# An RWKV-7 chunk scan in a two-layer hybrid mixer: the triangular inverse is folded into the keys, and a step has two links instead of three

## The chip, the cores and the metric

One Trainium2 chip, one of its cores. The metric is device time of one execution in microseconds; lower is better. All 512 tokens (256 of context, 256 latent, width 2048) go through two layers in one launch.

## The reference

Each layer normalises and modulates the tokens, projects them once, runs four token mixers in parallel (A and C are attentions, B is RWKV-7 in both directions, D is a gated DeltaNet in both directions), gates and projects each, sums them, and adds an output projection. The change touches mixer B, whose recurrence is

```python
def step(s, inp):
    r_t, w_t, k_t, v_t, kk_t, a_t = inp
    sa = jnp.einsum('bhij,bhj->bhi', s, -kk_t)
    s = (s * w_t[:, :, None, :] + sa[..., None] * (kk_t * a_t)[:, :, None, :]
         + v_t[..., None] * k_t[:, :, None, :])
    return s, jnp.einsum('bhij,bhj->bhi', s, r_t)
```

run over the context and then the latent tokens, forward and backward, for eight heads of 64, all in float32. The outputs of the context are needed in the first layer only.

## The kernel before

**Two kinds of TensorE work.** The large products (projections, branch merges, output projection) are split into high and low halves and run as 128x128 matmuls of 512 or 256 columns into PSUM tiles named `big`, with weights `wh`, `wl` that ScalarE and VectorE split from the loaded `wr`. These are the *fills*. They sit in a queue of generators, `s.queue`, and are drawn from it while other work is emitted. The planner is `small` (L259): each small matmul that the program emits reports a price in ns (`mm`, L282, and `turn`, L299), the price times `rho` is added to a debt, and as soon as the debt is above zero fills are emitted until it is paid and at least `QUANT` = 2600 ns of them stand there. A scheduler of the framework then sets the final order on each engine by dependences.

**The RWKV scan.** The tokens are cut into eight chunks of 64. Within a chunk the recurrence is solved with a unit triangular 64x64 inverse. Heads go in four pairs `j`; one head of a pair lies in partitions 0 to 63, the other in 64 to 127, so every tile holds both, and each 64x64 matmul uses one corner quarter of the array. For each pair and direction `d`, `b_stage1` (L886) builds per chunk: `ar` (decayed keys and receptances), the products `AT01`, `AT10`, `AT11` (L948 to 963), `tok0` and `tok1` (keys with tokens in the partitions, `tok2` L796) and the matrix to be inverted. `b_scan` (L971) then runs eight steps, one for a chunk, with the state `S`:

- link 1: `Z = AT10.vt + ar.S` in PSUM (tile `sc`), copied to SBUF by VectorE (L991);
- link 2: `U = E.Z` with the inverse `E` (tile `iR`), copied by VectorE (L997);
- link 3: `S' = wc * (tok1.vt + tok0.U) + wc * S`, VectorE L315 (L319 in the first step), the last term by ScalarE (`sw`, L309);
- beside these, the output is accumulated over the whole scan in a PSUM tile `acc`: `vt.AT11`, `S.ar`, `U.AT01`, for the chunks whose output is needed.

There are 4 pairs x 2 directions x 8 steps in each layer, 128 steps in all. Matmuls are written head by head (`for R in HS`).

**The inverse.** `inv_gen` (L704) is a generator that yields after each operation: 31 pairs of VectorE operations `it`, `iX` (L715, L717) on 32x32 blocks, two VectorE transposes `iE` and `iF` (L723, L725), 16 matmuls `iF,iL`, ScalarE copies to `iT` and POOL copies, 16 matmuls of `iT` and `iE`, ScalarE copies into `iR`. The inverse of the direction that comes next is run in the background of a scan: `bgstep(n)` (L677) advances it by n operations, after link 1, after link 2 and at the end of a step by `BG` = 3, 3, 4, and `bgstep(1000)` behind the scan finishes it. The DeltaNet mixer uses the same `inv_gen`.

Of the kernel before, what the change touches and what calls it, by code (L numbers as in the profile page):

```python
# [183 lines left out]
STEP = 1050.0  # L184
BG = (3, 3, 4, 10, 10)


class Kern:
    def __init__(s, tc, ins, out, dbg=None):
        s.tc, s.nc, s.i, s.out = tc, tc.nc, ins, out  # L190
        s.n = s.l = 0
        s.queue, s.done, s.debt, s.rho, s.filling, s.bg = [], set(), 0.0, 0.0, False, []
        s.side, s.sdebt, s.inside = None, 0.0, False
        s.wide, s.form = 0.0, (128, 128)


    def nm(s, t):
        s.n += 1
        return f"{t}_{s.n}"

    BUFS = {t: 2 for t in ("ar AT01 AT10 AT11 tok0 tok1 wc bo vt dl nb dec Dk ktok vs pT pt aq "
                           "iR sw po it").split()}
    BUFS.update(mr=16, Z=3, U=3, S=3, vs=3, dZ=3, Sd=4, Rb=16, po=3, ms=1, wr=5, wh=4, wl=4, QD=3, qg=3, dl=4, vn=2,
                nb=4, dec=4)
# [54 lines left out]
    def small(s, ns):  # L259
        if s.filling:  # L260
            s.wide += ns
            return
        if s.side and not s.inside:
            s.sdebt += ns * SIDE[s.l]
            while s.sdebt > 0 and s.side:
                s.sdebt -= STEP
                s.sidestep()
        s.debt += ns * s.rho
        if s.debt > 0:
            got = 0.0  # L270
            while s.queue and (s.debt > 0 or got < QUANT):
                s.pump()
                s.debt -= s.wide
                got += s.wide
# [7 lines left out]
    def mm(s, o, l, r, start=True, stop=True):  # L282
        s.nc.tensor.matmul(o, l, r, start=start, stop=stop)  # L283
        k, m, n = l.shape[0], l.shape[-1], int(np.prod(r.shape[1:]))
        if l.dtype == F32R:
            ns = max(n / 2.4 + 13, 107)
        elif k == m == 128:
            ns = max(4 * n / 2.4, 222)
        elif m == 32 and k == 128:
            ns = n / 2.4  # L290
        elif m <= 32:
            ns = 52
        elif k == m:
            ns = max(1.1 * n, 60)
        else:
            ns = max(1.3 * n, 110)
        s.small(ns + s.turn(max(32, k), max(32, m)))
# [406 lines left out]
    def inv_gen(s, pool, st, sign, grp, R, pair=False):  # L704
# [3 lines left out]
        nc = s.nc  # L708
        Bt, X, lo = st
        x = X.rearrange("p m i -> p i m")  # L710
# [18 lines left out]
        ps = s.bank()  # L729
# [23 lines left out]
        yield  # L753
        for D_, h, u0, u1, du, wE in out:
            up, dn = HQ[h]
            for u in range(u0, u1):
                if wE:
# [37 lines left out]

    def tok2(s, x, pool, tag):  # L796

# [3 lines left out]
        pv = ps.rearrange("p (m h f) -> p m h f", m=4, h=2)  # L801
        o = s.tl(pool, [128, 8, 64], tag)
        ov = o.rearrange("p (m e) f -> p m e f", e=2)
# [82 lines left out]
    def b_stage1(s, J, d):  # L886
# [59 lines left out]
        inv = s.inv_load(pool, ps)  # L946
        AT = [[None, None], [None, None]]
        for q, x in enumerate((bt, kt)):  # L948
            for e in range(1 - q, 2):
                AT[q][e] = s.tl(pool, [128, 8, 64], "AT%d%d" % (q, e))  # L950
            for g in range(2):
# [9 lines left out]
                for e in es:  # L961
                    mk = rep(s.c("bm", d * 128 + e * 64, d * 128 + e * 64 + 64), 4)
                    s.tt(AT[q][e][:, 4 * g:4 * g + 4, :], ps[:, :, e, :], mk, ALU.mult)
        tok = [s.tok2(x, pool, "tok%d" % q) for q, x in enumerate((bt, kt))]
        E = s.tl(pool, [128, 8, 64], "iR")
        J["d"][d] = (ar, AT, tok, E, wc)
        s.background(s.inv_gen(pool, inv, -1, [(0, 8, d == 1)], E))

    ORDER = [[0, 1, 2, 3, 4, 5, 6, 7], [3, 2, 1, 0, 7, 6, 5, 4]]

    def b_scan(s, J, d):  # L971
        nc = s.nc
        pool, t0 = s.bst["pool"], s.bst["t0"]
        c0 = t0 // 64
        ar, AT, tok, E, wc = J["d"][d]
        vt = J["vt"]
# [3 lines left out]
        yps = J["y"]  # L980
        pc = None
        S = None
        for st in range(8):
            c = s.ORDER[d][st]
            ps = s.scb((128, 64))
            for R in HS:
                s.mm(ps[R, :], AT[1][0][R, c, :], vt[R, c, :], True, st == 0)
                if st > 0:
                    s.mm(ps[R, :], ar[R, c, 0, :], S[R, :], False, True)
            Z = s.tl(pool, [128, 64], "Z")  # L990
            nc.vector.tensor_copy(Z, ps)  # L991
            s.bgstep(BG[0])
            ps = s.scb((128, 64))
            for R in HS:
                s.mm(ps[R, :], E[R, c, :], Z[R, :])
            U = s.tl(pool, [128, 64], "U")
            nc.vector.tensor_copy(U, ps)  # L997
            s.bgstep(BG[1])
            Sn = None
            if st < 7:  # L1000
                ps = s.scb((128, 64))
                for R in HS:
                    s.mm(ps[R, :], tok[1][R, c, :], vt[R, c, :], True, False)
                    s.mm(ps[R, :], tok[0][R, c, :], U[R, :], False, True)
                Sn = s.tl(pool, [128, 64], "S")
# [6 lines left out]
            if c >= c0:  # L1012
                for R in HS:
                    o = yps[R, c * 64:c * 64 + 64]
                    s.mm(o, vt[R, c, :], AT[1][1][R, c, :], d == 0 and c == c0, False)
                    if st > 0:
                        s.mm(o, S[R, :], ar[R, c, 1, :], False, False)
                    s.mm(o, U[R, :], AT[0][1][R, c, :], False, d == 1 and st == 7)
            s.bgstep(BG[2])
            S = Sn  # L1020
# [580 lines left out]
```

## Time and profile before

| | |
|---|---|
| median of 3 runs | 2846.87 us (2844.48 to 2854.17) |
| profiled execution | 2842.45 us |
| its span in the trace | 2840.7 us, mean granted clock 0.984 |
| RWKV scans of layer 0 | 244.9 to 737.0 us of the span |
| RWKV scans of layer 1 | 1803.0 to 2205.0 us of the span |

The span is that of the profiled execution, from the first to the last instruction in the trace. In the rows, PE is TensorE, DVE is VectorE, ACT is ScalarE, PEld a weight load. A name such as `sc<-Z,iR` says that a matmul wrote a tile `sc` from the tiles `Z` and `iR`; L283 is the line of the helper that records every matmul, so matmuls are told apart by their tiles. An fp32 matmul leaves two records. The end of a matmul's record is modelled, so what it costs is read from the distance of the starts.

### The profile page before, as it was taken

Reading aid. Unit: us, or ns where it says so; the run is one execution under the profiler, and the core shown is the slowest. Engines: PE = TensorE matmul, PEld = TensorE weight load, DVE = VectorE, ACT = ScalarE, POOL = GpSimd, SP = SyncE. Lnnn points to the kernel's source line nnn. Section 1 sums busy time; section 2 is a strip of 40 time slices with the busy share of each in tenths; the row PEclk is TensorE's granted clock in tenths of the full one; section 3 lists DMA queues with packets and bytes.
Section 4 is the critical chain, followed back from the end, with each engine's and each line's share of the span. In section 5 each row is a group of like instructions: output and inputs, shape, how many; then the busy total and the mean of one; then the engine's idle time right before and its main releaser. Section 6 shows DMA issues by size and latency. Waiting matters only on the chain. (4 is left out here: it accounts for less than half of the span.)

```text
span 2840.7 us, 52626 instructions
## 1 busy us (share of the span) xinstructions
PE 2710.4 (95%) x19438; PEld 2056.8 (72%) x19438; DVE 1856.9 (65%) x5255; ACT 1260.0 (44%) x2705; POOL 180.0 (6%) x436
## 2 busy tenths in 40 slices
PE   7998999999999998999999999999999999999897
PEld 3676666677787786777787756776777887867897
DVE  4337776656676777876553354777765687678775
ACT  3334333333354555655442244444443356455553
POOL 0000000000010101000000000010010001100000
PEclk9999999999999999999999999999999999999999
DMA  9753243322342323224537886322332442433465
GB/s 346 261 189 127 83 131 105 127 83 68 115 121 88 100 72 115 79 82 134 170 114 248 279 282 203 96 78 78 93 91 75 157 143 88 133 98 88 144 190 159
DMA packets 210049, 385.80 MB, mean 136 GB/s; under 512 B 24640, under 2 KB 37824, under 8 KB 209792
## 3 DMA queue, kind: packets, MB, share of 16 engines
q1 hardware_dynamic: 199872, 351.23, 39.6%
q0 software_dynamic: 9920, 31.20, 2.9%
q8 instruction: 153, 2.51, 0.4%
q14 instruction: 104, 0.85, 0.1%
HBM read 346.95 MB, written 35.39 MB: 135 GB/s over the span
## 5 line engine op out<-in xcount | busy, mean ns | idle before, releaser
L283 PE MATMUL big<-Rb,wh 128*128 128x512 f32 (+1 forms) x3280 | 1100.7, 364 | 21.3 <-ACT Rb L1325 10.0
L283 PE MATMUL big<-Ra,wh 128*128 128x512 f32 (+1 forms) x2128 | 777.3, 365 | 8.9 <-DVE po L315 5.6
L375 ACT CAST wh<-wr 128x512 fp32r<-128x512 f32 x712 | 438.8, 619 | 762.8 <-PE big L283 576.2
L283 PEld LDWEIGHTS big<-Rb,wh 128*128 128x128 f32 x3280 | 612.1, 191 | 128.8 <-ACT Rb L1325 14.0
L312 DVE TENSOR_TENSOR wl<-wr,wh 128x512 fp32r<-128x512 f32 x712 | 488.4, 688 | 304.3 <-ACT wh L375 280.3
L283 PE MATMUL big<-Ra,wl 128*128 128x512 f32 (+1 forms) x1616 | 597.2, 370 | 6.3 <-DVE wl L312 6.3
L283 PEld LDWEIGHTS big<-Ra,wh 128*128 128x128 f32 x2128 | 407.5, 192 | 84.3 <-issue 9.5
L283 PE MATMUL big<-Rb,wl 128*128 128x512 f32 (+1 forms) x1088 | 380.4, 350 | 1.1 <-DVE wl L312 1.1
L283 PEld LDWEIGHTS big<-Ra,wl 128*128 128x128 f32 x1616 | 310.3, 192 | 53.4 <-DVE wl L312 8.6
L283 PEld LDWEIGHTS big<-Rb,wl 128*128 128x128 f32 x1088 | 207.6, 191 | 26.2 <-DVE wl L312 1.5
L312 DVE TENSOR_TENSOR iX<-iX,it 128x60 f32<-128x60 f32 (+24 forms) x744 | 181.4, 244 | 15.7
L312 DVE TENSOR_TENSOR it<-iB,iX 128x60 f32<-128x60 f32 (+24 forms) x744 | 172.7, 232 | 15.6
L315 DVE SCALAR_TENSOR_TENSOR po<-po,big 128x512 f32<-128x512 f32 (+1 forms) x128 | 70.6, 552 | 77.1 <-PE big L283 74.2
L283 PE MATMUL big<-Rb,wr 128*128 128x256 f32 (+1 forms) x448 | 111.3, 417 | 5.0 <-ACT po L309 3.1
L309 ACT ACTIVATE sw<-S,wc 128x64 f32<-128x64 f32 x96 | 33.4, 348 | 176.2 <-DVE S L315 153.5
L283 PE MATMUL big<-mr,s 128*32 128x512 f32 x384 | 85.2, 617 | 18.3 <-DMA mr<-in_wmod 18.3
L309 ACT ACTIVATE po<-big,gb 128x512 f32<-128x512 f32 (+1 forms) x128 | 74.2, 579 | 57.3 <-PE big L283 41.2
L283 PEld LDWEIGHTS big<-Rb,wr 128*128 128x128 f32 (+1 forms) x448 | 70.6, 179 | 24.1 <-issue 7.3
L283 PE MATMUL sc<-vt,AT 64*64 64x64 f32 x512 | 71.3, 238 | 0.0
L315 DVE SCALAR_TENSOR_TENSOR cz<-raw,par,cz 128x508 f32<-128x508 f32 (+3 forms) x96 | 67.2, 700 | 5.4 <-ACT cz L309 5.0
L632 DVE TENSOR_REDUCE mx<-mx 128x1 f32<-128x512 f32 (+1 forms) x96 | 57.1, 599 | 18.7 <-PE mx L283 17.5
L283 PE MATMUL sc<-vt,tok 64*64 64x64 f32 x448 | 67.5, 232 | 0.0
(371 smaller groups left out, 4033.0 us busy)
## 6 DMA issues: line engine op xcount, KB each, us to landing
wr<-in_win SPq DMA_DIRECT2D x440, 256.0 KB, 2.7
mr<-in_wmod SPq DMA_DIRECT2D x320, 256.0 KB, 5.0
wr<-in_wbr SPq DMA_DIRECT2D x128, 256.0 KB, 2.7
wr<-in_wout SPq DMA_DIRECT2D x128, 256.0 KB, 3.1
wr<-in_wmod SPq DMA_DIRECT2D x64, 256.0 KB, 3.9
wr<-in_gup SPq DMA_DIRECT2D x64, 256.0 KB, 2.6
x<-in_xT SPq DMA_DIRECT2D x16, 256.0 KB, 5.4
po<-y SPq DMA_DIRECT2D x16, 256.0 KB, 3.0
```

The lines of the kernel that those rows point to most:

```text
L283: s.nc.tensor.matmul(o, l, r, start=start, stop=stop)
L309: s.nc.scalar.activation(o, i, f, bias=bias, scale=scale, **k)
L312: s.nc.vector.tensor_tensor(o, a, b, op)
L315: s.nc.vector.scalar_tensor_tensor(o, a, sc, b, op0, op1)
L375: s.nc.scalar.copy(hi, raw)
L632: nc.vector.tensor_reduce(mx[:, hc], ps[:, 0:nk], AX.X, ALU.max)
```

## The change

Since U is only used linearly, `tok0.U = (tok0.E).Z` and `U.AT01 = Z.(E.AT01)`. A new generator `b_fold` makes the inverse in the transposed form `F` (same tile name, `iR`), then multiplies it once into `TA`, a tile that holds `tok0` and `AT01` side by side: 16 matmuls of 64x64 by 128 columns for a pair and direction (64 columns for chunks without output), evicted by ScalarE into `TA` itself. A step then has two links: Z, and S straight from Z by `TA`. U, its copy and the product E.Z are gone. The matmuls of the two heads are written in turns, in the scan and in the second block of `inv_gen`. `held` keeps the planner from emitting fills except at two places of a step. The background inverse advances by 5 and 5 instead of 3, 3 and 4. The planner's price of a 64x64 matmul of n columns goes from 1.1 n (at least 60) to 0.85 n (at least 30) ns.

```diff
-BG = (3, 3, 4, 10, 10)
+BG = (5, 5, 0, 10, 10)
...
@@ small
-        if s.debt > 0:
+        if s.debt > 0 and not s.held:
@@ mm
-            ns = max(1.1 * n, 60)
+            ns = max(0.85 * n, 30)
@@ inv_gen
-        for D_, h, u0, u1, du, wE in out:
-            up, dn = HQ[h]
-            for u in range(u0, u1):
+        a, b = [[(u, wE) for _, g, u0, u1, _, wE in out if g == h for u in range(u0, u1)] for h in range(2)]
+        for z in zip(a, b):
+            for (up, dn), (u, wE) in zip(HQ, z):
                 if wE:
                     s.mm(p2[dn, u, :], T1[up, u, :], E[up, u, :])
                 else:
...
@@ b_stage1
-        AT = [[None, None], [None, None]]
+        TA = s.tl(pool, [128, 8, 2, 64], "TA")
+        AT = [[None, TA[:, :, 1, :]], [s.tl(pool, [128, 8, 64], "AT1%d" % e) for e in range(2)]]
...
-        tok = [s.tok2(x, pool, "tok%d" % q) for q, x in enumerate((bt, kt))]
-        E = s.tl(pool, [128, 8, 64], "iR")
-        J["d"][d] = (ar, AT, tok, E, wc)
-        s.background(s.inv_gen(pool, inv, -1, [(0, 8, d == 1)], E))
+        s.tok2(bt, pool, None, TA[:, :, 0, :])
+        tok1 = s.tok2(kt, pool, "tok1")
+        J["d"][d] = (ar, AT[1], TA, tok1, wc)
+        s.background(s.b_fold(pool, inv, d, TA, c0))
+
+    def b_fold(s, pool, inv, d, TA, c0):
+
+        F = s.tl(pool, [128, 8, 64], "iR")
+        yield from s.inv_gen(pool, inv, -1, [(0, 8, d == 0)], F)
+        for _ in range(5):
+            yield
+        for g in range(2):
+            w = 2 if 4 * g >= c0 else 1
+            ps = s.bank((128, 4, 2, 64))
+            for cc in range(4):
+                for R in (slice(0, 64), slice(64, 128)):
+                    s.mm(ps[R, cc, 0:w, :], F[R, 4 * g + cc, :], TA[R, 4 * g + cc, 0:w, :])
+            s.nc.scalar.copy(TA[:, 4 * g:4 * g + 4, 0:w, :], ps[:, :, 0:w, :])
+            yield
@@ b_scan
+            o = lambda R: yps[R, c * 64:c * 64 + 64]
+            s.held = True
             ps = s.scb((128, 64))
             for R in HS:
-                s.mm(ps[R, :], AT[1][0][R, c, :], vt[R, c, :], True, st == 0)
-                if st > 0:
+                s.mm(ps[R, :], AT[0][R, c, :], vt[R, c, :], True, st == 0)
+            if st > 0:
+                for R in HS:
                     s.mm(ps[R, :], ar[R, c, 0, :], S[R, :], False, True)
             Z = s.tl(pool, [128, 64], "Z")
             nc.vector.tensor_copy(Z, ps)
-            s.bgstep(BG[0])
-            ps = s.scb((128, 64))
-            for R in HS:
-                s.mm(ps[R, :], E[R, c, :], Z[R, :])
-            U = s.tl(pool, [128, 64], "U")
-            nc.vector.tensor_copy(U, ps)
-            s.bgstep(BG[1])
-            Sn = None
             if st < 7:
                 ps = s.scb((128, 64))
                 for R in HS:
-                    s.mm(ps[R, :], tok[1][R, c, :], vt[R, c, :], True, False)
-                    s.mm(ps[R, :], tok[0][R, c, :], U[R, :], False, True)
+                    s.mm(ps[R, :], tok1[R, c, :], vt[R, c, :], True, False)
+            if c >= c0:
+                for R in HS:
+                    s.mm(o(R), vt[R, c, :], AT[1][R, c, :], d == 0 and c == c0, False)
+                if st > 0:
+                    for R in HS:
+                        s.mm(o(R), S[R, :], ar[R, c, 1, :], False, False)
+            s.bgstep(BG[0])
+            s.held = False
+            s.small(0.0)
+            s.held = True
+            Sn = None
+            if st < 7:
+                for R in HS:
+                    s.mm(ps[R, :], TA[R, c, 0, :], Z[R, :], False, True)
                 Sn = s.tl(pool, [128, 64], "S")
...
             if c >= c0:
                 for R in HS:
-                    o = yps[R, c * 64:c * 64 + 64]
-                    s.mm(o, vt[R, c, :], AT[1][1][R, c, :], d == 0 and c == c0, False)
-                    if st > 0:
-                        s.mm(o, S[R, :], ar[R, c, 1, :], False, False)
-                    s.mm(o, U[R, :], AT[0][1][R, c, :], False, d == 1 and st == 7)
-            s.bgstep(BG[2])
+                    s.mm(o(R), Z[R, :], TA[R, c, 1, :], False, d == 1 and st == 7)
+            s.bgstep(BG[1])
+            s.held = False
+            s.small(0.0)
             S = Sn
```

The omitted rest lets `tok2` write into a given tile, sets `held` up and gives `TA` two buffers.

How instructions move, at three places. The first is one step of the last scan of layer 0 on TensorE, from Z to the next Z (`sc` and `acc` are the PSUM tiles of the links and the output, `big` the fills). Before:

```order
L283 MATMUL sc_7720<-Z_7718,iR_7196 64x64 x2
L283 MATMUL sc_7725<-vt_6234,tok_1661_7191 64x64
L283 MATMUL acc_7197<-AT_1649_7117,vt_6234 64x64
L283 MATMUL acc_7197<-ar_7012,S_7689 64x64
L283 MATMUL big_7592<-Ra_1536,wh_7759 128x512
L283 MATMUL sc_7725<-U_7723,tok_1659_7181 64x64
L283 MATMUL sc_7725<-vt_6234,tok_1661_7191 64x64
L283 MATMUL sc_7725<-U_7723,tok_1659_7181 64x64
L283 MATMUL acc_7197<-AT_1641_7076,U_7723 64x64
L283 MATMUL acc_7197<-AT_1649_7117,vt_6234 64x64
L283 MATMUL acc_7197<-ar_7012,S_7689 64x64
L283 MATMUL acc_7197<-AT_1641_7076,U_7723 64x64
```

After:

```order
L283 MATMUL sc_7417<-vt_5975,AT_1517_6777 64x64 x2
L283 MATMUL acc_6898<-AT_1518_6778,vt_5975 64x64 x2
L283 MATMUL big_7439<-Ra_490,wl_7443 128x512
L283 MATMUL sc_7417<-S_7411,ar_6715 64x64 x2
L283 MATMUL sc_7424<-vt_5975,tok_1536_6893 64x64 x2
L283 MATMUL acc_6898<-ar_6715,S_7411 64x64 x2
L283 MATMUL big_7439<-Ra_498,wh_7442 128x512
L283 MATMUL sc_7424<-Z_7422,TA_6776 64x64 x2
L283 MATMUL acc_6898<-TA_6776,Z_7422 64x64 x2
L283 MATMUL big_7439<-Rb_499,wh_7442 128x512
```

The two matmuls with U into `sc` and into `acc` are gone, the row of `Z,iR` has become one of `Z,TA`, and rows that named one head at a time now come as x2, one for each head.

The second place is the end of an inverse in layer 1 on TensorE (`iF,iL` and the product of `iE` and `iT` are its two blocks of matmuls, `wr`, `wh` and `wl` are weights of fills). Before, where the first `sc<-Z,iR` follows 36 rows below the last one shown:

```order
L283 MATMUL mx_20788<-iF_20765,iL_20311 32x32 x16
L283 MATMUL mx_20934<-cst_87,raw_20932 128x2 x4
L283 MATMUL big_21019<-Rb_17702,wr_21017 32x512
L283 MATMUL big_21019<-Rb_17710,wr_21017 32x512
L283 MATMUL big_21019<-Rb_17718,wr_21017 32x512
L283 MATMUL big_21019<-Ra_17725,wr_21017 32x512
L283 MATMUL mx_20788<-iE_20764,iT_20789 32x32 x16
L283 MATMUL big_21019<-Ra_17733,wr_21017 32x512
```

After:

```order
L283 MATMUL mx_21178<-iF_21167,iL_20770 32x32 x16
L283 MATMUL big_21640<-Ra_17557,wl_21853 128x512
L283 MATMUL big_21640<-Ra_17565,wh_21852 128x512
L283 MATMUL big_21640<-Rb_17566,wh_21852 128x512
L283 MATMUL big_21640<-Ra_17565,wl_21853 128x512
L283 MATMUL mx_21178<-iE_21166,iT_21179 32x32 x16
L283 MATMUL big_21640<-Ra_17573,wh_21852 128x512
L283 MATMUL big_21640<-Rb_17574,wh_21852 128x512
L283 MATMUL big_21640<-Ra_17573,wl_21853 128x512
L283 MATMUL mx_21257<-TA_20781,iR_20879 64x64 x8
L283 MATMUL mx_21267<-TA_20781,iR_20879 64x128 x8
L283 MATMUL mx_21299<-raw_21295,cb_17958 128x256
L283 MATMUL sc_21568<-Z_21566,TA_20781 64x64 x2
```

Behind the inverse now stand the two groups of the fold, `mx<-TA,iR`, and right behind them the first link of the scan that reads it.

The third place is VectorE in a step of a scan in layer 0, from Z to the next link (`it` and `iX` are the steps of the background inverse). Before:

```order
L991 COPY Z_7321<-sc_7297 128x64
L312 TENSOR_TENSOR iX_7074<-iX_7074,it_7368 128x15x5
L312 TENSOR_TENSOR it_7376<-iB_7072,iX_7074 128x70
L312 TENSOR_TENSOR iX_7074<-iX_7074,it_7376 128x14x5
L312 TENSOR_TENSOR it_7412<-iB_7072,iX_7074 128x65
L312 TENSOR_TENSOR iX_7074<-iX_7074,it_7412 128x13x5
L312 TENSOR_TENSOR it_7415<-iB_7072,iX_7074 128x60
L312 TENSOR_TENSOR iX_7074<-iX_7074,it_7415 128x12x5
L997 COPY U_7331<-sc_7328 128x64
```

After:

```order
L1010 COPY Z_6936<-sc_6931 128x64
L312 TENSOR_TENSOR it_7000<-iB_6772,iX_6774 128x63
L312 TENSOR_TENSOR iX_6774<-iX_6774,it_7000 128x21x3
L312 TENSOR_TENSOR it_7003<-iB_6772,iX_6774 128x60
L312 TENSOR_TENSOR iX_6774<-iX_6774,it_7003 128x20x3
L312 TENSOR_TENSOR it_7006<-iB_6772,iX_6774 128x76
L312 TENSOR_TENSOR iX_6774<-iX_6774,it_7006 128x19x4
L312 TENSOR_TENSOR it_7017<-iB_6772,iX_6774 128x72
L312 TENSOR_TENSOR iX_6774<-iX_6774,it_7017 128x18x4
L312 TENSOR_TENSOR it_7020<-iB_6772,iX_6774 128x68
L315 SCALAR_TENSOR_TENSOR S_6973<-sc_6938,wc_6026,sw_6974 128x64
```

The next link's operation is the copy of U before and the S of the step after; seven operations of the inverse stood between, and now nine do.

## Rows read from the trace of the kernel before

**Rows 1.** The page, part 1: busy us, share of span, instructions by engine.

```profile
PE 2710.4 (95%) x19438; PEld 2056.8 (72%) x19438; DVE 1856.9 (65%) x5255; ACT 1260.0 (44%) x2705; POOL 180.0 (6%) x436
```

**Rows 2.** Windows of both layers' scans: us, busy (x) by engine, PEclk, DMA.

```profile
244.90:737.00 492.10, 481.00 (x4492) 332.34 (x4491) 322.59 (x1032) 170.75 (x375) 34.09 (x76) 0.99 0.32 101
1803.00:2205.00 402.00, 393.85 (x3957) 294.95 (x3958) 281.66 (x946) 167.99 (x379) 35.24 (x78) 0.97 0.28 84
```

**Rows 3.** Waits of TensorE, whole span: total us, times, longest.

```profile
PE mx L283 <- DVE iF L725: 18.6, 8, 4.7
...
PE sc L283 <- DVE Z L991: 0.9, 1, 0.9
```

**Rows 4.** Order of time, TensorE, 708.3 to 712.1: start, us, instruction.

```profile
708.50 0.27 PE L283 MATMUL sc<-S,ar 64*64 64x64 f32 x1
708.50 0.27 PE L283 MATMUL sc<-vt,AT 64*64 64x64 f32 x1
708.60 0.22 PE L283 MATMUL sc<-S,ar 64*64 64x64 f32 x1
...
708.67 0.28 PE L283 MATMUL sc<-S,ar 64*64 64x64 f32 x2
708.88 0.50 PE L283 MATMUL big<-Rb,wh 128*128 128x512 f32 x1
709.21 0.39 PE L283 MATMUL big<-Ra,wl 128*128 128x512 f32 x1
709.44 0.40 PE L283 MATMUL big<-Ra,wh 128*128 128x512 f32 x1
...
709.90 0.40 PE L283 MATMUL big<-Ra,wl 128*128 128x512 f32 x1
710.23 0.33 PE L283 MATMUL sc<-Z,iR 64*64 64x64 f32 x4
710.40 0.28 PE L283 MATMUL sc<-vt,tok 64*64 64x64 f32 x2
710.51 0.28 PE L283 MATMUL acc<-AT,vt 64*64 64x64 f32 x2
```

**Rows 5.** Windows of one scan in each layer, columns as in rows 2.

```profile
705.30:734.28 28.98, 28.93 (x286) 19.60 (x283) 8.54 (x27) 5.78 (x12) 0.54 (x1) 1.00 0.19 56
2176.66:2201.72 25.06, 25.06 (x251) 18.44 (x248) 8.69 (x26) 6.45 (x14) 1.08 (x2) 1.00 0.26 74
```

**Rows 6.** Order of time, TensorE, 2064.5 to 2066: fills of 256 columns.

```profile
2064.85 0.28 PE L283 MATMUL big<-Ra,wl 128*128 128x256 f32 x1
2064.97 0.28 PE L283 MATMUL big<-Ra,wh 128*128 128x256 f32 x1
```

**Rows 7.** Order of time, TensorE, 269.9 to 273: both blocks of one inverse.

```profile
269.98 0.69 PE L283 MATMUL mx<-iF,iL 32*32 32x32 f32 x32
...
271.73 1.09 PE L283 MATMUL mx<-iT,iE 32*32 32x32 f32 x32
```

**Rows 8.** Order of time, TensorE, 320 to 345: 16 matmuls of 128 columns.

```profile
337.10 1.96 PE L283 MATMUL mx<-ar,E 64*64 64x128 f32 x32
```

**Rows 9.** Lines by form, ScalarE: count, busy us, mean ns, idle before.

```profile
L658 ACT COPY pT<-mx 128x512 f32<-128x512 f32 x32 | 18.6, 582 | 7.4 <-PE mx L305 6.7
```

**Rows 10.** Lines by form, VectorE, columns as in rows 9.

```profile
L997 DVE COPY U<-sc 128x64 f32<-128x64 f32 x128 | 28.5, 223 | 49.9 <-PE sc L283 48.2
...
L312 DVE TENSOR_TENSOR it<-iB,iX 128x60 f32<-128x60 f32 x72 | 18.0, 250 | 1.8
```

**Rows 11.** Waits of TensorE in layer 1's scans, columns as in rows 3.

```profile
PE mx L283 <- DVE iF L725: 5.1, 4, 3.3
```

**Rows 12.** Order of time, all engines, 433 to 436: iF and its reader.

```profile
433.29 0.45 DVE L725 STREAM_TRANSPOSE iF<-iE 128x256 f32<-128x256 f32 x1
...
435.13 0.43 PE L283 MATMUL mx<-iF,iL 32*32 32x32 f32 x14
```

**Rows 13.** Window behind the longest of these waits, columns as in rows 2.

```profile
1805.00:1817.30 12.30, 12.30 (x100) 10.16 (x96) 6.21 (x13) 7.26 (x16) 1.52 (x4) 0.50 0.33 110
```

More of the change, by code (lines that the diff above doesn't have):

```diff
@@ L193, in __init__ @@
         s.side, s.sdebt, s.inside = None, 0.0, False
-        s.wide, s.form = 0.0, (128, 128)
+        s.wide, s.form, s.held = 0.0, (128, 128), False
     def nm(s, t):
@@ L199, in nm @@
         return f"{t}_{s.n}"
-    BUFS = {t: 2 for t in ("ar AT01 AT10 AT11 tok0 tok1 wc bo vt dl nb dec Dk ktok vs pT pt aq "
+    BUFS = {t: 2 for t in ("ar TA AT10 AT11 tok1 wc bo vt dl nb dec Dk ktok vs pT pt aq "
                            "iR sw po it").split()}
@@ L794, in inv_gen, with tok2 @@
                 s.act(R[H0, u0:u1, 64:128], ps[H0, u0:u1, :], AF.Copy, float(-sign))
-    def tok2(s, x, pool, tag):
+    def tok2(s, x, pool, tag, o=None):
         ps = s.bank()
@@ L801, in tok2 @@
         pv = ps.rearrange("p (m h f) -> p m h f", m=4, h=2)
-        o = s.tl(pool, [128, 8, 64], tag)
+        if o is None:
+            o = s.tl(pool, [128, 8, 64], tag)
         ov = o.rearrange("p (m e) f -> p m e f", e=2)
@@ L946, in b_stage1 @@
         inv = s.inv_load(pool, ps)
-        AT = [[None, None], [None, None]]
+        TA = s.tl(pool, [128, 8, 2, 64], "TA")
+        AT = [[None, TA[:, :, 1, :]], [s.tl(pool, [128, 8, 64], "AT1%d" % e) for e in range(2)]]
         for q, x in enumerate((bt, kt)):
-            for e in range(1 - q, 2):
-                AT[q][e] = s.tl(pool, [128, 8, 64], "AT%d%d" % (q, e))
             for g in range(2):
@@ L974, in b_scan @@
         c0 = t0 // 64
-        ar, AT, tok, E, wc = J["d"][d]
+        ar, AT, TA, tok1, wc = J["d"][d]
         vt = J["vt"]
@@ L980, in b_scan @@
         yps = J["y"]
-        pc = None
         S = None
```

## The prediction

> **What bounds the kernel now.** I began with the page's busy shares: TensorE is busy 95% of the span, VectorE 65%, ScalarE 44% [rows 1]. So anything that takes time off TensorE shows, and anything taken off another engine shows only where TensorE waits for it. The edit lies in the RWKV scans, so the next view was the two stretches that hold them, 492 us in layer 0 and 402 us in layer 1, 894 us together [rows 2]: there TensorE is busy 98%, VectorE 66 and 70%, ScalarE 35 and 42%. The third view was TensorE's waits [rows 3]. The dependent links of the scan, which one would think the reason for shortening a step from three links to two, cost TensorE almost nothing: its largest total wait for one of them is 0.9 us, for Z, in the whole program. The background inverse costs more, 18.6 us in eight waits for iF. So a shorter chain is worth nothing by itself here, because fills stand between the links. What can be won is TensorE time: fewer small matmuls, better paired ones, and fewer places where they cut into the fills.
>
> The last view was the order of time on TensorE, which prices these [rows 4]. A 64x64 fp32 matmul shows as two records. Records of the two heads (upper and lower half of the partitions) start together: at 708.50 two stand beside each other. One head's matmuls that stand alone follow at 0.11 to 0.12 us (710.40 to 710.51), so a matmul costs 117 ns alone and half, 58.5 ns, when its twin of the other head runs beside it. A fill of 512 columns follows the one before it at 0.23 us (709.21 to 709.44; 0.227 over long runs). An **interruption** of the fills by small matmuls costs more than its matmuls: the first small one starts 0.33 us after the last fill (709.90 to 710.23), 0.10 too late; the first two records are 0.10 apart (708.50 to 708.60), 0.04 too much; the last record of a stretch is at 708.73 (the second of the x2), and the fill comes at 708.88, 0.09 too late; and the next fill follows after 0.33 (708.88 to 709.21), 0.10 too late. Together 0.33 us.
>
> **The scan's matmuls.** With these prices I split one scan of each layer, both free of inverse work on TensorE [rows 5]; of the 286 and 251 records there, four stand at the edges and are left out. Layer 0: 28.98 us hold 60 fills (13.6 us), 20 interruptions (6.6) and 111 small matmuls (222 records), for which 8.8 us are left: 79 ns each. Layer 1: 25.06 us hold 25 fills of 512 columns and 48 of 256 (0.12 us each, [rows 6]), 11.4 us, 22 interruptions (7.3) and 87 matmuls in 6.4 us: 73 ns each. So the order of before, head by head, already runs half beside each other. By the order listing the scans issue 960 small matmuls in layer 0 and 784 in layer 1, afterwards 832 and 656: the 256 of E and Z are gone. Before: 960 x 79 + 784 x 73 ns = 133.0 us. After, heads strictly in turn, 1488 x 58.5 ns = 87.0 us. The difference is **-46.0 us**, of which 128 x 117 ns = 15.0 us is the removed link and the rest turn-taking. If turn-taking paired them only as well as now, 1488 matmuls at 76 ns would leave -20; that is the other bound.
>
> This rests on two heads running side by side although both write one PSUM tile, as in the rows at 708.50 (both into sc). The Trainium skill, "TensorEngine Tiling (Array Packing)", section "Gotcha 1: PSUM Pressure", states the opposite: different row tiles cannot access the same PSUM bank simultaneously. By that rule the alternating matmuls would queue at the price of lone ones; the trace disagrees with its equal starts at 708.50, so the row decides, and what the rule would give stands with the rivals.
>
> **The inverse halves.** Where the heads alternate, 32 records take 0.69 us; where eight of one head stand before eight of the other they take 1.09 [rows 7]. The second block of the inverse now alternates: 16 inverses x 0.40 = 6.4 us, and for the eight of the DeltaNet, which only partly have this shape, 0.2 us each: **-8.0 us** (bounds -6.4 and -9.6).
>
> **The fold.** New are 128 pairs of matmuls F x TA, 96 pairs of 128 columns and 32 of 64. The nearest row is the same shape, 16 matmuls, so eight pairs, of 128 columns in 1.96 us [rows 8], less the 0.16 us by which the last one's record outlasts its slot: 0.225 us a pair. 96 x 0.225 + 32 x 0.117 = **+25.3 us**. Its evictions on ScalarE, 24 of 128x512 at 0.58 us [rows 9] and 8 of half that, add 17 us to 339 of 894 busy [rows 2]: hidden, since the second group's matmuls and fills stand behind the first group's. If that cover were gone, half of the 32 would be on the path, 9 us.
>
> **The interruptions.** The planner holds the fills to two places in a step instead of three or four. Counted in the order listing, stretches of small matmuls between fills fall from 211 to 160 in layer 0's scans and from 221 to 164 in layer 1's: 108 fewer, x 0.33 = **-35.6 us** (0.23 if a quarter to a third of the loss stays with the longer stretches: -25). The planner's lower price for a small matmul also lets 222 fills leave the scans for later places; the fills are the same in number and cost the same there, so I take nothing for them. No DMA and no POOL operation is added or moved past another; the weight loads follow the fills.
>
> So far -64.3 us.
>
> **What VectorE does with it.** 128 copies of U go, 223 ns each [rows 10]: 28.5 us that nobody waited for, so nothing directly. But the inverse that VectorE computes for the next direction now has to be *folded* before that direction's first Z,TA, and TensorE gets there sooner. In layer 1, four of the eight inverses already make TensorE wait, 5.1 us together, 3.3 of it once [rows 11]. TensorE's scan there shortens by 3.8 us (per scan, matmuls 2.3, interruptions 2.4, inverse 0.4, fold back 1.4), VectorE's only by its eight U copies, 1.8 us. So up to 2.0 us of every scan's gain can turn into a wait: 8 x 2.0 = 16 us. In layer 0 the room is larger, 1.4 us after iF's end at the tightest I looked at (433.74 to 435.13, [rows 12]); with 4.1 us gained and 1.8 given by VectorE I take 0.7 us for seven inverses, 5 us. Behind that the order has only three or four fills between iF,iL and iE,iT, and three between that and the fold; ScalarE's copies between them just about fit, and I take 0.2 us at 15 places, 3 us. Together **+24 us**. The bounds are 0 (VectorE's queue runs ahead, as it does where TensorE keeps it waiting: 48.2 us ahead of the 128 copies of U [rows 10]) and 15 x 3.3 us, the longest such wait in these scans [rows 11], 50 us.
>
> That longest wait has a tail: after it, from 1805.0 to 1817.3, the granted clock is 0.50, the 1.2 GHz level [rows 13]. A tail of 12.3 us at half speed costs 6 us. I take two thirds of one more, **+4 us** (0 to 14).
>
> **Sum.** -46.0 - 8.0 + 25.3 - 35.6 + 24 + 4 = -36.3 us. The profiled execution took 2842.45 us, 1.75 more than its span, so it would come to 2806. The median of the runs is 4.4 us above it; on that scale I predict **2811 us**.
>
> **Rivals.** A change under 0.3%, 8.5 us, can't be told from none in this kernel.
>
> *The inverse stays hidden.* VectorE, relieved of U, finishes in time, and the term of 28 us falls away: 2846.87 - 64.3 = 2783. For it: 30 to 34% of VectorE is free. Against it: four waits in layer 1 already. Chance 0.12.
>
> *The inverse takes all.* Every one of 15 inverses makes TensorE wait 3.3 us, 50 us, with tails of 14: 64 of 64 are gone, 2847, within 0.3%. For it: fold and inverse now stand in a row with few fills between. Against it: the 3.3 us is the largest of eight. Chance 0.12.
>
> *Slower: the queue of VectorE.* Five inverse operations of about 0.25 us ([rows 10]) are now issued per link, where it were three or four, 3.3 on average, and the order listing has as many as nine between a Z and its S: on average a result leaves VectorE 0.4 us later. Between a link's last matmul and the first that waits for it stand two pairs (0.23), an interruption (0.33) and at least one or two fills (0.23 each), 0.8 to 1.0 us; the link itself needs 0.28 for the last record and 0.23 for the copy. That leaves 0.3 to 0.5 us for the queue. It decides when what is queued takes more than that in most links. If 224 links then expose 0.25 us each, 56 us come back on top of the forecast's -36: 2867. Against it: VectorE waits for TensorE ahead of the U copies, 48.2 us in all [rows 10], so its queue is often empty. Chance 0.07.
>
> *Heads don't run side by side in one bank.* At 117 ns each, 1488 matmuls cost 174.1 us instead of 133.0 (+41), the fold 50.6, the inverse gains nothing, and -35.6 remains: 2903. The rows at 708.50 speak against it. By the rule of the Trainium skill named above it would come out so. Chance 0.01.
>
> That the links aren't really removed can be left out: the order listing holds no U.
>
> **The numbers.** The forecast keeps 0.68; its own range is 2796 to 2830, from the bounds of the interruption term (+10), the inverse waits (+-12) and turn-taking (some +10). All of it is faster by over 0.3%. Faster: 0.68 + 0.12 = 0.80. Same: 0.12. Slower: 0.07 + 0.01 = 0.08. The range goes from 2782 to 2848, so that half of either middle rival (0.06 each) and the slower ones (0.08) lie outside: 0.20.
>
> **What would show it.** In the profile after: a small matmul of the scan costs about 60 ns in such windows, instead of 73 to 79, and the records of the two heads start in pairs throughout; TensorE's waits on iF, and new ones on TA or Z behind the fold, grown from 5 to about 25 us in the scans; the two scan stretches shorter by some 36 us in all once the fills moved out are counted back. It would be wrong if TensorE waited for Z or S by more than a few us (then VectorE's queue is the bound), if the granted clock stood at 0.50 for more than one or two further stretches, or if the waits for iF stayed at 5 us and the time fell below 2790.

## The result and the profile after

The changed kernel takes 2815.43 us (median of 4 runs, 2803.45 to 2820.73), the kernel before, measured beside it, 2845.68. The medians are 30 us apart; the ratio, which goes by the means, is 0.9882, with a 95% interval of 0.9843 to 0.992: a gain of 1.2%, some 33 us. Forecast were 2811 us.

The profiled execution took 2812.09 us, its span is 2810.3. Part 1 of its page (to be read against [rows 1]; instructions of each engine, busy us and share):

```profile
PE 2667.1 (95%) x19438; PEld 2035.5 (72%) x19438; DVE 1834.1 (65%) x5127; ACT 1277.1 (45%) x2737; POOL 180.0 (6%) x436
```

TensorE is busy 43.3 us less and the span is 30.4 us shorter, so it stands idle for 12.9 us more: 143.2 us instead of 130.3. VectorE lost its 128 copies, ScalarE gained 32 evictions and 17 us, as worked out. The mean clock of each run stands in the view of the cores (span and mean granted clock of TensorE); before it was 0.984:

```profile
core 0: 2810.3 us, clock 0.976
```

These two views split the result. Idle time is span less busy time. What the clock cost is about (1 - mean granted clock) x span, if a microsecond at half clock does half a microsecond's work: 45.5 us before, 67.4 after. (Rows for that stand below: fills of 512 columns follow each other at 0.43 us where the clock is 0.50, against 0.23.) What is left of the busy time is **TensorE's work at full clock**: 2710.4 - 45.5 = 2664.9 us before, 2667.1 - 67.4 = 2599.7 after. So the change takes 65.2 us of work off TensorE, and gives back 12.9 in idle time and 21.9 in clock: -30.4. The forecast was -64.3, +24 and +4.

The split is less sure than its decimals. The kernel before was run 27 more times beside the later experiments, with granted clocks of 0.976 to 0.981, never 0.984. By those its clock cost 59.8 us in the mean, and its idle time and work together came to 2777 to 2789 us, where its profiled execution has 2795.2. The changed kernel's four runs have 68.9 and 2743.1. By all these runs the change takes 41.9 us off idle time and work together and gives back 9.1 in clock. So what is said below of work, idle time and clock against the kernel before, from its one profile, can be wrong by some 10 us. For every other kernel here, idle time and work together in the profile lie within 6 us of the mean of its runs.

What TensorE waits for (total us, times, longest; [rows 3] and [rows 11] before):

```profile
PE mx L283 <- DVE iF L725: 35.3, 19, 4.7
...
PE sc L283 <- DVE Z L1010: 3.6, 4, 1.4
```

The waits for iF have nearly doubled from 18.6 us, and those for a link remain small. The same view of the scans alone, first of layer 0 (248.6 to 674 us), then of layer 1 (1775.5 to 2165.7):

```profile
PE mx L283 <- DVE iF L725: 4.0, 5, 1.4
```

```profile
PE mx L283 <- DVE iF L725: 15.2, 8, 2.8
```

Every one of layer 1's eight inverses now makes TensorE wait, and five of layer 0's. Before, it was four of layer 1's, for 5.1 us [rows 11]. The clock in the two scans (windows; columns as in [rows 2]: us, then busy time of PE, PEld, DVE, ACT, POOL, then PEclk) and in three of the stretches at such waits, the first of them behind an inverse of the DeltaNet:

```profile
248.60:674.00 425.40, 409.27 (x4321) 287.39 (x4316) 299.58 (x947) 168.38 (x370) 31.61 (x73) 1.00 0.34 106
1775.50:2165.70 390.20, 372.67 (x3925) 284.89 (x3926) 274.91 (x899) 172.14 (x391) 36.04 (x77) 0.94 0.28 83
```

```profile
1062.80:1083.30 20.50, 15.85 (x127) 11.82 (x128) 9.69 (x31) 9.10 (x23) 5.13 (x15) 0.50 0.39 116
2035.60:2056.10 20.50, 19.93 (x163) 14.28 (x164) 5.04 (x22) 4.09 (x10) 3.46 (x8) 0.50 0.15 46
2141.40:2151.70 10.30, 10.07 (x110) 7.53 (x110) 1.46 (x4) 3.34 (x8) 2.06 (x5) 0.50 0.24 69
```

Layer 0's scans are 67 us shorter than before, but 156 of their fills left for later places (by the listing, 1000 before, 844 now), some 35 us; layer 1's clock fell from 0.97 to 0.94. The three stretches, of 20.5, 20.5 and 10.3 us, stand at 0.50, the 1.2 GHz level; they begin late in waits of 3.63, 2.75 and 2.37 us for iF. In the trace's record of the clock, nine of the 15 stretches at 0.50 begin within 2 us of such a wait, 92 us in all; before it was five of 13, 44 us. This is the order of time around the last of the three (all engines; start, us, and in brackets idle time and its releaser):

```profile
2141.17 0.41 DVE L725 STREAM_TRANSPOSE iF<-iE 128x256 f32<-128x256 f32 x1
...
2141.63 1.06 PE L283 MATMUL mx<-iF,iL 32*32 32x32 f32 x32 [2.37 <-DVE iF L725]
...
2142.74 0.74 ACT L744 COPY iT<-mx 32x256 f32<-32x256 f32 x2 [4.72 <-PE mx L283]
...
2143.22 0.63 PE L283 MATMUL big<-Rb,wh 128*128 128x512 f32 x1
...
2143.65 0.63 PE L283 MATMUL big<-Ra,wl 128*128 128x512 f32 x1
...
2144.63 1.07 PE L283 MATMUL mx<-iT,iE 32*32 32x32 f32 x32
...
2147.20 2.83 PE L283 MATMUL mx<-TA,iR 64*64 64x64 f32 x32
...
2149.82 0.42 PE L283 MATMUL sc<-Z,TA 64*64 64x64 f32 x4
```

The chain of the inverse, iF, two blocks, fold and first link, is complete 8 us after iF, and TensorE waits only at its head: the few fills in between cover ScalarE's copies. And these rows, from a scan without inverse work, show the price of the new order (TensorE, order of time):

```profile
2156.13 0.33 PE L283 MATMUL sc<-S,ar 64*64 64x64 f32 x4
2156.30 0.28 PE L283 MATMUL sc<-vt,tok 64*64 64x64 f32 x4
2156.51 0.50 PE L283 MATMUL big<-Rb,wh 128*128 128x512 f32 x1
2156.84 0.40 PE L283 MATMUL big<-Ra,wl 128*128 128x512 f32 x1
2157.17 0.33 PE L283 MATMUL sc<-Z,TA 64*64 64x64 f32 x4
2157.34 0.28 PE L283 MATMUL sc<-vt,AT 64*64 64x64 f32 x4
2157.55 0.50 PE L283 MATMUL big<-Ra,wh 128*128 128x512 f32 x1
```

Rows come as x4 now: two heads of two records each. The 12.51 us from the fill at 2152.45 to the one at 2164.96 hold 20 fills of 512 columns (4.5 us), 12 interruptions (4.0, at the price of before) and 66 small matmuls, for which 4.0 us are left: 61 ns each, where [rows 5] gave 73. The 16 matmuls of one fold of layer 0 take 1.9 us, as their neighbour in [rows 8]:

```profile
648.91 1.92 PE L283 MATMUL mx<-TA,iR 64*64 64x128 f32 x32
```

### The profile page after: what moved, and what is told of

Same layout as the page of the kernel before. It is cut to its first block, busy times and chain, and to the rows that moved or that the text cites. A ratio compares the mean times of both kernels' runs of the same rounds, so it can differ in the third digit from the quotient of the medians.

```text
span 2810.3 us, 52526 instructions
## 1 busy us (share of the span) xinstructions
PE 2667.1 (95%) x19438; PEld 2035.5 (72%) x19438; DVE 1834.1 (65%) x5127; ACT 1277.1 (45%) x2737; POOL 180.0 (6%) x436
## 5 line engine op out<-in xcount | busy, mean ns | idle before, releaser
L309 ACT ACTIVATE po<-big,gb 128x512 f32<-128x512 f32 (+1 forms) x128 | 74.0, 578 | 68.5 <-PE big L283 52.7
L632 DVE TENSOR_REDUCE mx<-mx 128x1 f32<-128x512 f32 (+1 forms) x96 | 57.0, 598 | 20.8 <-PE mx L283 19.9
L283 PE MATMUL mx<-pT,avt 128*64 128x128 f32 x640 | 62.1, 292 | 1.5 <-ACT pT L658 1.3
L305 PE MATMUL mx<-cst,pt 128*128 128x128 f32 x320 | 52.9, 286 | 7.8 <-ACT pt L309 7.5
```

The lines of the kernel that those rows point to most:

```text
L305: s.nc.tensor.transpose(o, i, s.c("id"))
L309: s.nc.scalar.activation(o, i, f, bias=bias, scale=scale, **k)
L632: nc.vector.tensor_reduce(mx[:, hc], ps[:, 0:nk], AX.X, ALU.max)
```

## The experiments

My theory: TensorE's work sets the time, by three terms (heads in turns -39; the removed link, its interruptions and the fold together -25), and VectorE's inverse with the clock behind it gives some back. The rivals: the shorter chain is what pays; or the hold on the fills; or VectorE's queue takes over. For all runs the split of above, from page and view of the cores of the profiled execution (in us; the kernel before was measured again beside each set, 2845.7 to 2847.1; a run's median and its profiled execution differ by up to 14 us). The last two columns go by span and clock of every run of a kernel: what the clock cost in the mean, and what is left of the span, idle time and work together.

| kernel | median | ratio, interval | idle | clock cost | work | clock cost, all runs | idle and work, all runs |
|---|---|---|---|---|---|---|---|
| before | 2845.7 to 2847.1 | | 130.3 | 45.5 | 2664.9 | 59.8 | 2785.0 |
| the change | 2815.4 | 0.9882 (0.9843 to 0.992) | 143.2 | 67.4 | 2599.7 | 68.9 | 2743.1 |
| turns_only | 2811.8 | 0.9881 (0.9858 to 0.9905) | 123.3 | 56.2 | 2630.2 | 57.6 | 2753.3 |
| turns_held | 2821.5 | 0.9916 (0.9891 to 0.9941) | 128.0 | 67.6 | 2620.4 | 73.4 | 2747.7 |
| after_heads | 2845.6 | 0.9995 (0.9979 to 1.0012) | 140.3 | 88.4 | 2621.4 | 80.8 | 2763.0 |
| after_bg10 | 2798.1 | 0.9817 (0.9788 to 0.9847) | 128.0 | 41.7 | 2612.8 | 56.6 | 2736.7 |
| after_bg10_gap | 2811.0 | 0.9888 (0.9866 to 0.9911) | 142.3 | 53.2 | 2602.0 | 70.3 | 2738.7 |
| turns_gap | 2822.5 | 0.9922 (0.9896 to 0.9948) | 126.1 | 59.1 | 2629.9 | 68.5 | 2754.0 |
| after_gap7 | 2811.7 | 0.9888 (0.9858 to 0.9918) | 139.3 | 67.3 | 2598.6 | 77.4 | 2735.3 |
| after_unheld | 2787.1 | 0.9794 (0.9779 to 0.9808) | 128.9 | 55.7 | 2602.0 | 54.3 | 2731.5 |
| unheld_price | 2802.9 | 0.9847 (0.9829 to 0.9865) | 130.5 | 64.4 | 2605.5 | 61.6 | 2739.8 |
| unheld_price_bg10 | 2813.4 | 0.9881 (0.9862 to 0.99) | 135.2 | 67.4 | 2606.6 | 68.2 | 2742.6 |
| after_short | 2715.2 | 0.9539 (0.9525 to 0.9553) | 99.3 | 21.7 | 2589.5 | 26.5 | 2687.4 |
| turns_short | 2750.5 | 0.9661 (0.9647 to 0.9676) | 93.3 | 19.2 | 2634.5 | 22.0 | 2726.7 |

**One part alone: the turns.** Kernel before, `b_scan` with one loop over the heads for each operand, and the `zip` in `inv_gen`:

```diff
             for R in HS:
                 s.mm(ps[R, :], AT[1][0][R, c, :], vt[R, c, :], True, st == 0)
-                if st > 0:
+            if st > 0:
+                for R in HS:
                     s.mm(ps[R, :], ar[R, c, 0, :], S[R, :], False, True)
...
                     s.mm(ps[R, :], tok[1][R, c, :], vt[R, c, :], True, False)
+                for R in HS:
                     s.mm(ps[R, :], tok[0][R, c, :], U[R, :], False, True)
```

> The kernel before with the heads written in turns in the scan's matmuls and in the second block of the inverse; three links, planner and background as before. Theory (TensorE time by pairing): 1744 small matmuls at 58.5 instead of 76 ns, -31 us, and the inverse -8, the same number of interruptions (432 stretches): 2846 - 39 = 2807, up to 2820 if waits for the inverse give some back. Rival (the gain comes from the shorter chain): no change, 2843 to 2850. Rival (one bank serialises the heads): slower, 2880 or more.

2811.8 us: the order of the heads alone gives as much as the whole change. Work falls by 34.7 us against the profile of before (39 expected), and idle time and work together by 32 over all runs; part 1 of its page and its clock:

```profile
PE 2686.4 (96%) x19438; PEld 2031.8 (72%) x19438; DVE 1854.1 (66%) x5255; ACT 1259.3 (45%) x2705; POOL 179.7 (6%) x436
```

```profile
core 0: 2809.7 us, clock 0.980
```

These 35 us don't come from a shorter chain, since here the chain is as long as before. And two heads in one PSUM bank don't hold each other up, or the turns would have made it slower. The rule of the Trainium skill, "TensorEngine Tiling (Array Packing)", section "Gotcha 1: PSUM Pressure", that different row tiles cannot access the same PSUM bank simultaneously, does not hold for these tiles: the equal starts at 708.50 [rows 4] and the 35 us speak against it.

**All but the fold.** turns_only with the hold, set free in three places, and the lower price:

```diff
+            s.held = False
+            s.small(0.0)
+            s.held = True
             ps = s.scb((128, 64))
             for R in HS:
                 s.mm(ps[R, :], E[R, c, :], Z[R, :])
```

> Everything of the change but the fold and the removed link: heads in turns, fills held (to three places, since three links remain), the lower price of a small matmul. U and its link stay; the listing has 428 stretches in the scans. Theory: as turns_only, 2805 to 2820; against the changed kernel it lacks the 108 interruptions (-36) and E.Z (-15) but also the fold (+25) and much of the new waiting for iF, so that the two should come within 15 us of each other. Rival (shorter chain): near 2840, 25 us above the changed kernel.

2821.5 us, a little above the stated span, and 6 us from the changed kernel. Fold and removed link, with the background's 5 and 5 that came with them, are worth 21 us of work between the two (2620.4 to 2599.7) and 6 in time, which the intervals don't tell apart: idle time takes 15.2 of it. Hold and lower price together make it 10 us slower than turns_only.

**The turns undone.** The changed kernel with the loops over heads outermost again where that can be (Z, two of three output products, second block of the inverse):

```diff
             for R in HS:
                 s.mm(ps[R, :], AT[0][R, c, :], vt[R, c, :], True, st == 0)
-            if st > 0:
-                for R in HS:
+                if st > 0:
                     s.mm(ps[R, :], ar[R, c, 0, :], S[R, :], False, True)
```

> The changed kernel with the heads one after the other again in Z, in the output products and in the second block of the inverse (fold and links stay). Theory: the inverse costs 8 us more, and the 900 or so matmuls written head by head some 10 to 18 us more: 2815 + 18 to 26 = 2833 to 2841. Rival (the order of heads does not matter, TensorE looks ahead): 2815 plus at most 8.

2845.6 us, no faster than the kernel before, and above the stated 2833 to 2841. Work rises by 21.7 us, inside the 18 to 26; over all its runs idle time and work together rise by 20 and the clock's cost by 12, and for the clock I had put nothing.

**The inverse sooner.**

```diff
-BG = (5, 5, 0, 10, 10)
+BG = (10, 10, 0, 10, 10)
```

> The changed kernel with 10 and 10 background operations a step instead of 5 and 5, so that the inverse is done after about half a scan. Theory (what the change gave back is the wait for iF, 35 us in 19 waits, and the half clock behind it): waits for iF fall by 15 us or more, less time at the 0.50 clock, 2785 to 2805. Rival (VectorE's queue binds): ten operations stand ahead of Z and S, TensorE waits for Z and S by 20 us or more, 2830 to 2870.

2798.1 us, in the stated span, but not for the stated reason. Waits for iF are as long as they were, though ten operations ahead of each Z and S make TensorE wait little for Z (5.0 us) and S, so that VectorE's queue is not the bound:

```profile
PE mx L283 <- DVE iF L725: 35.2, 19, 6.6
...
PE sc L283 <- DVE Z L1010: 5.0, 5, 1.4
```

What fell, in an execution that is the quicker by 14 us than the median, is other idle time and the clock's cost, 41.7 us instead of 67.4 (56.6 instead of 68.9 over all runs). The matmuls of iF move forward in TensorE's order along with iF. The next three runs tried to part them.

```diff
-        for _ in range(6):
+        for _ in range(20):
             yield
         ps = s.bank()
```

> The changed kernel with 10 and 10 background operations a step, and 20 instead of 6 empty background steps between the transpose iF and its matmuls, so that these matmuls come about a step later in TensorE's order. after_bg10 showed iF still waited for (35 us in 19 waits), because the matmuls move forward with it. Theory (waits for iF and the half clock behind them are what the change gives back): waits for iF fall from 35 to below 15 us, time at the 0.50 clock from 87 to 60 us or less, 2765 to 2790. Rival (VectorE's queue): the waits reappear at Z and S, 2798 or more.

> The changed kernel with 7 and 7 background operations a step and 20 empty steps behind iF. The inverse ends about six steps into the scan. Theory: between after_bg10_gap and the changed kernel, waits for iF 15 to 25 us, 2785 to 2805, unless the fold then comes too late for the next scan, which would show as waits for TA or Z. Rival (VectorE's queue): faster than after_bg10_gap, since fewer operations stand ahead of Z and S.

> Three links (no fold) with heads in turns as in turns_only, background 7, 7, 6 a step and the same 20 empty steps behind iF. Tells what the fold is worth once the inverse makes nobody wait. Theory: turns_only's 2812 less its waits for iF and their half clock, 2785 to 2802; after_bg10_gap is 15 to 30 us faster (108 interruptions -36, E.Z -15, fold +25). Rival (the removed link is worth nothing): both within 8 us of each other.

All three miss: 2811.0 (BG 10, 10, 0), 2811.7 (7, 7, 0) and 2822.5 us (7, 7, 6). The first lies where the rival had put it, at 2798 or more, but the rival's sign, waits that reappear at Z and S, is weak: those for Z are 9.2 us. In after_bg10_gap the waits for iF are 27.5 us in 17, in turns_gap 20.9 in 13. In after_bg10_gap the matmuls of 23 of the 24 iF still start within 0.15 us of iF's end, although the program puts them later. My reading, which no run shows by itself, is that the framework's scheduler places them where it expects iF, and that on the chip VectorE is later than that. What program order can't do, less work for VectorE should (24 of the 31 pairs of each inverse are left out):

```diff
+            if k % 4 == 3:
                 s.tt(tm, b, x[:, k:k + 1, 0:w].to_broadcast([128, n, w]), ALU.mult)
             yield
```

> The changed kernel with 24 of the 31 VectorE pairs of each inverse left out (only every fourth is computed, so the inverse is not one; the places of the matmuls in the program stay). VectorE has some 265 us less to do and iF comes early. Theory (the change's -64 us of TensorE work is there, and waits for iF and half clock give half of it back): waits for iF from 35 to below 10 us, clock back to 0.984 or better, and since the listing has 260 stretches in the scans instead of 324, another -21: 2815 - 25 - 22 - 21 = 2747, 2740 to 2775. Rival (the waits are made by TensorE's order, not by VectorE): no less waiting, 2790 to 2800.

> turns_only (three links, heads in turns) with the same 24 of 31 pairs left out. Tells what removing the link is worth when VectorE makes nobody wait. 411 stretches in the scans. Theory: turns_only's 2812 less 7 for stretches, 18 for waits and some 10 for the clock, 2770 to 2785, so 20 to 45 us above after_short. Rival (the removed link is worth nothing): within 10 us of after_short.

(and the same in front of the subtraction into iX). VectorE is 236 us less busy. Waits for iF in after_short, and its clock:

```profile
PE mx L283 <- DVE iF L728: 5.2, 4, 1.9
```

```profile
core 0: 2710.5 us, clock 0.992
```

2715.2 us, lower than the 2740 to 2775 that I expected: idle time falls by 43.9 us and the clock's cost by 45.7, twice what I had put there, work by 10 where I had put 21 (fewer stretches). For 20 of the 24 inverses the matmuls of iF now start 1 to 17 us behind iF. So idle time and half clock that go with VectorE's part of the inverse were some 90 us of the changed kernel, 30 of them waits for iF; how much of the rest comes from other VectorE work that gets its turn sooner is not shown. turns_short, with three links, takes 2750.5, below its 2770 to 2785. The two are 35 us apart, within the stated 20 to 45; the work differs by 45. That is the price of removed link, fold, hold and lower price together, since turns_short has none of them.

**The hold.**

```diff
-            s.held = True
+            s.held = False
```

> The changed kernel with the hold on the fills switched off everywhere in the scan (the flag stays false). The listing has 159 and 168 stretches in the scans, against 160 and 164 with it. Theory (the interruptions fell because a link fell away, not because fills are held): 2815 within 8 us. Rival (the hold makes the difference): 2830 to 2850.

(The flag stays false at both places where `b_scan` sets it.) A miss on the good side: 2787.1 us, 28 us faster than the changed kernel (intervals 0.9779 to 0.9808 against 0.9843 to 0.992) and the fastest of the kernels that leave nothing out. The hold is no part of the gain, it costs 28 us. TensorE's work is the same within the error, 2602.0, and so are the stretches in the listing, 159 and 168 against 160 and 164: the interruptions fell because a link fell away. Without the hold there are 14 us less idle time and 12 us less of clock. Its scans, in the same view as above:

```profile
250.30:682.00 431.70, 418.09 (x4342) 294.79 (x4338) 299.43 (x949) 168.73 (x373) 33.42 (x74) 0.99 0.34 106
1767.90:2144.40 376.50, 361.48 (x3929) 275.68 (x3928) 273.93 (x894) 171.76 (x391) 36.24 (x77) 0.98 0.29 86
```

Layer 1's scans stand at 0.98 instead of 0.94 and take 13.7 us less, with two more fills in them by their places in the trace. Yet the waits for iF are nearly as long as with the hold:

```profile
PE mx L283 <- DVE iF L725: 33.7, 16, 6.6
```

**More cover on top.** after_unheld with the old price, and then also with BG = (10, 10, 0, 10, 10):

```diff
-            ns = max(0.85 * n, 30)
+            ns = max(1.1 * n, 60)
```

> after_unheld (2787) with the planner's old price of a small matmul, 1.1 n and at least 60 ns, so that fills stay in the scans (1069 instead of 868 in layer 0 by the listing, 331 stretches instead of 327). Theory (TensorE waits less for the inverse when more fills stand in its scans): waits for iF 5 to 15 us less than after_unheld's 34, 2770 to 2787. Rival (only the number of stretches and matmuls counts): 2782 to 2792.

> The same with 10 and 10 background operations a step (306 stretches by the listing). Theory: both measures that gave the inverse more time together, and 25 stretches fewer (-8): 2760 to 2785. Rival (VectorE's queue, ten operations ahead of Z and S): waits for Z and S above 15 us, 2790 or more.

Both miss: 2802.9 and 2813.4. Waits for iF do fall, to 22.7 and 21.6 us from 33.7, as the theory wanted, but all idle time is as long as in after_unheld or longer, and the clock costs 9 and 12 us more. So the waits for iF alone don't rank these versions. The second lies in its rival's range, 2790 or more, but its waits for Z and S, 7.8 us, are half of what the rival needed.

Put in a row, these kernels take the change apart step by step, by medians: the turns -35 us (2847.0 to turns_only's 2811.8); fold and removed link, with the background's 5 and 5, another -9 (to unheld_price's 2802.9, which has neither hold nor lower price; each of its four runs is faster than each of turns_only's, though the intervals overlap a little); the lower price -16 (to after_unheld's 2787.1); the hold +28 (to the changed kernel's 2815.4). The other way round it comes out alike: with three links hold and lower price are +10, and fold and removed link then -6. In the step of -9, work falls by 24.7 us, and idle time (+7.2) and clock (+8.2) take back 15.4.

## Why the prediction was right, and where not

**What bounds the kernel.** Right. TensorE's waits for a link cost next to nothing, 0.9 us for Z before and 3.6 after; a kernel with the old chain and the new order of heads is as fast.

**Scan matmuls and inverse halves, -46.0 and -8.0.** 39 us of these 54 belong to turn-taking, and turns_only takes 34.7 us of work away by the profiles and is 35 us faster. The 58.5 ns that rest on two records starting side by side came out at 61.

**Fold and interruptions, +25.3 and -35.6, with the 15 us of E.Z.** Together -25.3; the work of the changed kernel against turns_only is -30.5, but in time the two are level, since idle time takes back 19.9 and the clock 11.2. The reason that I gave for the interruptions was wrong in part: it is not that the planner holds the fills, but that a step has one link less. By the listings, three links have 432 stretches without the hold (turns_only) and 428 with it (turns_held), two links 327 and 324.

**Hold and lower price, nothing.** I gave the hold no cost of its own and took nothing for the fills that the lower price moves out of the scans. The runs give +28 and -16 us. These two, and the -9 of fold and removed link, add up to +3; my own terms beside the turns, -25.3, +24 and +4, also come to +3. That is luck: the parts are not the same.

**What VectorE does with it, +24.** TensorE's idle time grew by 12.9 us, its waits for iF in the scans by 14.1 (5.1 to 19.2): 15.2 where I had put 16 new ones on top of 5.1 in layer 1, 4.0 where I had put 5 in layer 0. The place was right, the size some 10 us too large, as far as this one profile of before goes. I had also misread the room in layer 0: I looked at one inverse with 1.4 us, but in the trace of before the matmuls at 320.7 and 365.5 us start 0.05 and 0.42 us after their iF. And the fold is not the only cause: without the hold the waits for iF in both scans are 13.2 us instead of 19.2. (The four terms of a scan's 3.8 us add up to 3.7.)

**The clock, +4.** Too small: +21.9 between the two profiles, some +9 over all runs, which is inside my 0 to 14. I took two thirds of one more stretch at 0.50; layer 1's scans now have five such stretches, 47.8 us, where they had two, 20.5 us; each of the five begins within 2 us of a wait of 1.6 to 2.8 us for iF, and one at the DeltaNet's inverse at 1063.8 lasts 20.5 us. By my own test (0.50 for more than one or two further stretches) this part was wrong. By the profiles it did not show in the time because the idle time came out lower by 11 us and the work by 1.

My test on the scans came out: they are 78.5 us shorter together, of which some 40 are fills that moved out by their places in the trace, so 38 where I had put 36. So the mechanism of the turns and TensorE's share were right, and 36 us forecast against 33 measured owes something to errors of opposite sign. The rival in which the inverse takes all comes nearest to what became of the removed link: against turns_only, idle time and clock took back all of it.

**What stays open.** Why versions with the same work differ by 28 us in waits and clock, and so why the hold costs what it does. Whether background steps of 3, 3 and 4 would do better or worse with two links, since no run parts them from the fold. Where TensorE stands still, and where the clock falls behind that, changes with every shift of the scheduler's order; none of the knobs tried moved it as intended.

## What to carry to other kernels

Where small matmuls of two heads share the array, write them in turns, operand by operand: here it was worth 35 us, as much as the whole change, and cost nothing. A shorter chain paid here, on a busy engine, through fewer small matmuls and fewer places at which they cut into the long work (some 21 to 31 us of TensorE's work), not through its latency, and most of that came back as waits and clock. When a change has several parts, undo them one at a time: here one of them, the hold, cost almost as much as the best of them gained. And split a result into work, idle time and clock, from the page's first part and the mean granted clock, before explaining it, with the clock of several runs and not of one.

## What the runs showed of the hardware

The clock's part can be as large as the idle time that goes with it. In the changed kernel's four runs the mean granted clock goes with the time, 0.980 at 2803 us and 0.972 at 2821; and when most of VectorE's inverse was left out, the clock gave back as much, 45.7 us (42 over all runs), as the idle time itself, 43.9. My forecast had put the clock at a sixth of the waits.

Records of 64x64 matmuls of two heads start side by side although both write one PSUM bank, 58.5 to 61 ns for each against 117 ns alone.
